# Two k steps of the modulation matmuls between hand-overs, where one was made

## The chip, the cores and the metric

One core of a Trainium2 chip runs the whole program. The metric is the device time of one execution in microseconds (us). The kernel before took 1104.37 us, the median of three runs (1100.53 to 1105.21).

## The reference, cut to what matters

Two layers of a diffusion backbone over 256 latent and 256 context tokens of width 1024. Each layer computes

- a modulation: `mod = silu(c) @ w_mod[l] + b_mod[l]`, the same for `c_ctx`; `w_mod[l]` is 1024 x 6144, and the result is cut into six vectors `sh1, sc1, g1, sh2, sc2, g2`;
- `h = rmsnorm(x) * (1 + sc1) + sh1`, one combined input projection, then attention (8 heads) and a chunked SSD scan side by side, an output projection, and `x + g1 * o`;
- `h2 = rmsnorm(x) * (1 + sc2) + sh2`, a router, 32 experts of which two are used per token, and `x + g2 * y`.

In the second layer only the latent tokens go on. A final norm closes it. All data are float32.

## The kernel before, in words

**Modulation.** The vectors `sh1` and `sc1` of a layer are made by `mod_norm1`. The other four are made by `mod_group`, two groups per layer (`i` = 1 gives `g1, sh2`; `i` = 2 gives `sc2, g2`). A group contracts over 1024 in eight k steps. A k step is one 1 MB chunk of `w_mod` (128 x 2048) and four matmuls (line 303), one for each 512 columns, into four strips of 32 partitions of one PSUM bank (`md`, one buffer). A float32 matmul leaves two records in the trace, so a step is eight records, and the 32 steps of the kernel are 256. After the eighth step the bias is added (line 307), the result goes to DRAM, and four transposes (line 316) bring it into columns.

**Generators.** `mod_group` is a generator: after each k step it yields, with its estimated cost 0.94, and the caller decides what is emitted next. There are three callers' ways.

- `weave` (line 335) runs several generators together and always advances the one whose summed cost over its weight is least. In both layers the attention (`g_att`), the SSD (`g_ssd`) and the modulation (`mods`) are woven so (line 991), with weights 70, 28, 28 in layer 0 and 45, 15, 18 in layer 1. In layer 0 all its modulation groups are in this weave: two of `mod_group` and then `mod_norm1` of layer 1.
- `take(mods, n)` (line 348) advances it n yields. Layer 1 uses it: one, one and three yields (`EARLY - 2`) while its first norm waits for the last sums of the layer before (lines 521, 528, 546), and then `MBULK[n]` yields after each yield of the `bulk` generator (line 984), which makes the projections: `MBULK` is 1 at n = 0, 2, 4, 6 and 8, and 0 elsewhere.
- what is left in layer 1 goes into its weave.

So in layer 1 the five `take` yields are the steps k = 0 to 4 of its first group, the five of `MBULK` are k = 5, 6, 7, the bias and the transposes, and the eight steps of its second group are in the weave.

**Where the chunks lie.** Chunks k = 0 to 4 of layer 1's first group (`EARLY = 5`) are loaded early into large buffers (`wm`). The next five chunks of layer 1 (`MSMALL = 5`) are loaded by `qload` as four 256 KB quarters into small buffers whose tags are given by `MTAGS` ("pppt" and "tyyx"); these are tags that attention and SSD use as well. `chunk(k + 1, True)` asks for such a chunk one step ahead. All other chunks are loaded by `rload` into the tag `wh`, which has four buffers of 1 MB (`WHB = 4`).

**The four `wh` buffers.** The projections' weights are split into a high and a low part (`split_next`, lines 381 and 382: ScalarE makes the high part, VectorE the low one), and each such pair takes two of the four `wh` buffers. `weights(i)` at the head of each pair of blocks asks for the pair after the next. `bulk` goes through six blocks of `xbc` (three pairs) and then two passes of `z` (a pair each). After it, `wkv` and `wq` (lines 986, 987) take `wh` buffers, and hold them to the end of the attention.

**What sets the order.** The framework orders each engine's instructions when the program is built: it goes by program order, takes what its own time estimate says is ready, and gives a freed buffer to the one that asked first. `pin(...)` keeps some instructions in program order; inside `manual_schedule` the listed engines keep the order written. DMAs are issued on SyncE's queue (SP), in order; one that waits for a buffer holds up those behind it.

Of the kernel before, what the change touches and what calls it, by code (L numbers as in the profile page):

```python
# [82 lines left out]
def _tile_kernel(tc, A, out, dbg=None):  # L83
    nc = tc.nc
    pin = tc.keep_in_program_order
    V, S, G, T = nc.vector, nc.scalar, nc.gpsimd, nc.tensor
# [21 lines left out]
    def tp():  # L108
        return psT.tile([128, 512], F32, tag="tp", name="tp")

    def md_():
        return psM.tile([128, 512], F32, tag="md", name="md")
# [10 lines left out]
    def tw(tag, bufs, name, dt=F32):  # L123
        return P.tile([128, 512], dt, tag=tag, name=name, bufs=bufs)
# [9 lines left out]
    def rload(src, shape, t=None, after=None):  # L134
        n = 1
        for s in shape[1:]:
            n *= s
        v = (wh("wl") if t is None else t)[:, :n]
        if after is not None:
            V.tensor_copy(v[:, 0:1], after)  # L140
        d = nc.sync.dma_start(v, src)
        if pinned[0]:
            pin(d)
        if len(shape) == 3:
            v = v.rearrange("p (a b) -> p a b", a=shape[1])
        return v
# [15 lines left out]
    csT = kc[:, KC_A:KC_A + 256].rearrange("p (k m) -> p k m", k=8)  # L162
# [51 lines left out]
    def mod_norm1(l, pre=()):  # L214
        a1 = cp.tile([128, 2, 8], F32, tag="a1", name="a1", bufs=2)
        b1 = cp.tile([128, 2, 8], F32, tag="b1", name="b1", bufs=2)
        modT[l, "a1"], modT[l, "b1"] = a1, b1
        for b in range(8):
            w = pre[b] if b < len(pre) else rload(A["wm0"][l, b], [128, 8, 256], big("wm") if pre else None)
            pm = md_()  # L220
            for k in range(8):
                g = k % 4
                T.matmul(pm[32 * g:32 * g + 32, 0:256], csT[:, k, :], w[:, k], start=(k < 4), stop=(k >= 4))
            mr = tw("bm", 2, "mr")[:, 0:256]
            V.tensor_copy(mr, pm[:, 0:256])
            yield 0.9
            pt = tp()
            for s in range(2):
                T.matmul(pt[:, 2 * s:2 * s + 2], mr[:, s * 128:(s + 1) * 128], kcs("sel"), start=True, stop=True)
            V.tensor_scalar(b1[:, :, b], pt[:, 0:2], cps("bsh", l)[:, b:b + 1], None, op0=ALU.add)  # L230
            V.tensor_scalar(a1[:, :, b], pt[:, 2:4], cps("bsc", l)[:, b:b + 1], 1.0, op0=ALU.add, op1=ALU.add)
            V.tensor_scalar(a1[:, :, b], a1[:, :, b], cps("n1g", l)[:, b:b + 1], None, op0=ALU.mult)
            yield 0.1

    def qload(src, tags, after=None):
        q = []
        for n, a in enumerate(tags):
            if a == "o":
                t = kcs("rope")
            elif a == "k":  # L240
                t = kd[:, 0:512]
            elif a == "w":
                t = ke[:, 0:512]
            elif a == "l":
                t = kc[:, KC["le"][0]:KC["le"][0] + 512]
            elif a == "s":
                t2 = sm([128, D], "sact")
                t = t2[:, 0:512]
            elif a == "a":
                t = t2[:, 512:1024]  # L250
            else:
                tag, bufs = QUARTER[a]
                t = P.tile([128, 520], F32, tag=tag, name="we", bufs=bufs)[:, 0:512] if a == "q" else tw(tag, bufs, "we")
            if after is not None:
                G.tensor_copy(t[:, 0:1], after)
            nc.sync.dma_start(t, src[:, n * 512:(n + 1) * 512])
            q.append(t)
        return q
# [10 lines left out]
    def mod_group(l, i, pre=()):  # L269
        if i == 0:  # L270
            yield from mod_norm1(l)
            return
        pm = md_()
        q = {}

        def chunk(k, ahead=False):
            if k not in q and k < 8:
                src = A["wmod"][l, i - 1, k]
                if k < len(pre):
                    q[k] = [pre[k][:, g * 512:(g + 1) * 512] for g in range(4)]  # L280
                elif l and nmod[0] < MSMALL:
                    q[k] = qload(src, MTAGS[k % 2])
                    nmod[0] += 1
                elif not ahead:
                    w = rload(src, [128, 2048])
                    q[k] = [w[:, g * 512:(g + 1) * 512] for g in range(4)]
            return q.get(k)

        for k in range(8):
            if k == BMK:  # L290
                bm = tw("bm", 2, "bm")
                pin(G.memset(bm, 0.0))
                for who in range(2):
                    pin(nc.scalar.dma_start(bm[who:who + 97:32, :], A["bmod"][l, i]))
                if i == 2:
                    n2 = tw("bm", 2, "n2")
                    pin(G.memset(n2, 0.0))
                    for who in range(2):
                        pin(nc.scalar.dma_start(n2[who:who + 33:32, :], A["n2r"][l]))
            w = chunk(k)  # L300
            chunk(k + 1, True)
            for g in range(4):
                T.matmul(pm[32 * g:32 * g + 32, :], csT[:, k, :], w[g],
                         start=(k == 0), stop=(k == 7))
            yield 0.94
        mr = bm
        V.tensor_tensor(mr, pm, bm, op=ALU.add)
        if i == 2:
            V.scalar_tensor_tensor(mr[0:64], mr[0:64], 1.0, n2[0:64], op0=ALU.add, op1=ALU.mult)
        dt_ = dp.tile([128, 512], F32, tag=f"modd{l}{i}", name=f"modd{l}{i}")  # L310
        nc.gpsimd.dma_start(dt_[:], mr)
        modd[l, i] = dt_
        yield 0.01
        pt = tp()
        for b in range(4):
            T.transpose(pt[:, b * 128:(b + 1) * 128], mr[:, b * 128:(b + 1) * 128], ident)
        pv = pt.rearrange("p (b s h r) -> p r s h b", b=4, s=2, h=2)
        sec, nm = ((1, "sh2"), (0, "a2"))[i - 1]
        d = cp.tile([128, 2, 8], F32, tag=nm, name=nm)
        modT[l, nm] = d  # L320
        for who in range(2):
            V.tensor_copy(d[:, who].rearrange("p (h b) -> p h b", h=2), pv[:, who, sec])
        yield 0.5
# [38 lines left out]
    def mixer(l):  # L362
# [4 lines left out]
        pinned[0] = PINM[l]  # L367
        early = [rload(A["wmod"][l, MODS[l][0][1] - 1, k], [128, 2048], big("wm")) for k in range(EARLY * l)]
        mods = chain(*[mod_group(*m, early if i == 0 else ()) for i, m in enumerate(MODS[l])])
        hT, hH, hL, xn = [], [], [], []  # L370
        wsrc = [A["wt"][l, 0], A["wt"][l, 1], A["wxbc"][l, 2], A["wxbc"][l, 0], A["wxbc"][l, 1], A["wz"][l, 0], A["wz"][l, 1]]
# [1606 lines left out]
```

## Time and profile before

| | |
|---|---|
| median of three runs | 1104.37 us |
| the profiled execution's own time | 1102.8 us |
| its span | 1101.0 us |
| TensorE (PE) busy | 1009.9 us, 92% |
| VectorE (DVE) busy | 608.9 us, 55% |
| ScalarE (ACT), GpSimd (POOL) busy | 334.8 us, 355.0 us |
| mean granted TensorE clock | 0.968 |
| DMA moved | 306.21 MB, 278 GB/s mean |

The stages in the trace: projections of layer 0 up to about 118 us; its weave to about 256; its output projection, router and experts to about 634; layer 1's norm and projections to 718; its weave to about 800; then its output projection, router and experts to the end. In a timeline row the columns are start, duration, engine, line, operation, tile written <- tiles read, shapes, and the number of instructions merged; a bracket gives idle time of the engine ahead of it and what ended it.

### The profile page before, as it was taken

The numbers are of one execution on the slowest core, as the hardware profiler recorded it, in microseconds if no ns is written. First come the engines' busy times: TensorE is split into PE (matmuls) and PEld (weight loads), VectorE is DVE, ScalarE is ACT, GpSimd is POOL, SyncE is SP. The second block draws the span as 40 slices with busy tenths as digits, with TensorE's granted clock in tenths as the row PEclk, the third lists the DMA queues.
The fourth block names the chain that finished last, engine by engine and source line by source line (L and its number), as shares of the span: only waits on it lengthen the run. The fifth ranks groups of instructions, "written<-read, shape, count | busy, mean of one in ns | idle before, by whom it ended". The sixth has DMA issues, their size and how long they took to land. (4 is left out here: it accounts for less than half of the span.)

```text
span 1101.0 us, 14498 instructions
## 1 busy us (share of the span) xinstructions
PE 1009.9 (92%) x5244; PEld 558.0 (51%) x5244; DVE 608.9 (55%) x1351; ACT 334.8 (30%) x688; POOL 355.0 (32%) x366
## 2 busy tenths in 40 slices
PE   5999999999996999999699889999997999899986
PEld 3778554667674344344244357845775344323321
DVE  4596288875785356556445677749864153222222
ACT  4464344544630111111012075434642111101101
POOL 2130134420562467667636431023311011111121
PEclk9999999999986999999899899999997999999998
DMA  9521577787287997999979164475679699898971
GB/s 375 180 77 52 206 261 257 248 335 311 97 295 293 368 367 318 415 418 404 382 283 418 43 235 155 151 288 212 244 269 329 238 388 420 337 372 356 420 265 39
DMA packets 54675, 306.21 MB, mean 278 GB/s; under 512 B 6168, under 2 KB 7064, under 8 KB 22976
## 3 DMA queue, kind: packets, MB, share of 16 engines
q1 hardware_dynamic: 49120, 288.10, 67.0%
q0 software_dynamic: 4224, 15.21, 4.5%
q10 hardware_dynamic: 1248, 1.86, 0.5%
q8 instruction: 44, 0.72, 0.3%
q14 instruction: 39, 0.32, 0.1%
HBM read 300.89 MB, written 4.26 MB: 277 GB/s over the span
## 5 line engine op out<-in xcount | busy, mean ns | idle before, releaser
L1678 POOL TENSOR_TENSOR xs<-xs,tmp 128x512 f32<-128x512 f32 x144 | 180.2, 1281 | 276.4 <-DVE tmp L1677 276.3
L1610 PE MATMUL bk<-we,xgT 128*64 128x512 f32 (+1 forms) x950 | 242.1, 602 | 0.0
L1610 PEld LDWEIGHTS bk<-we,xgT 128*64 128x64 f32 (+1 forms) x950 | 62.7, 125 | 130.4 <-issue 127.9
L1647 PE MATMUL sc<-we,sa 128*64 128x512 f32 (+1 forms) x430 | 106.2, 600 | 0.1
L1663 DVE SCALAR_TENSOR_TENSOR yl<-sc,gs,yh 128x512 fp32r<-128x512 f32 x46 | 34.3, 748 | 113.2 <-ACT yh L1662 112.6
L1662 ACT ACTIVATE yh<-sc,gs 128x512 fp32r<-128x512 f32 x46 | 31.5, 687 | 210.9 <-PE sc L1647 167.7
L1647 PEld LDWEIGHTS sc<-we,sa 128*64 128x64 f32 (+1 forms) x430 | 31.1, 125 | 58.0 <-issue 56.7
L1677 DVE TENSOR_TENSOR tmp<-md,g 128x512 f32<-128x512 f32 x60 | 41.3, 688 | 29.7 <-POOL xs L1678 18.7
L1677 DVE TENSOR_TENSOR tmp<-py,g 128x512 f32<-128x512 f32 x60 | 41.2, 687 | 24.0 <-PE py L1674 13.2
L1616 ACT ACTIVATE sa<-bk 128x256 f32<-128x256 f32 x24 | 9.2, 383 | 136.1 <-PE bk L1610 126.8
L1578 PEld LDWEIGHTS tp<-PT,h 128*128 128x128 f32 x256 | 33.9, 199 | 28.4 <-issue 12.7
L1578 PE MATMUL tp<-PT,h 128*128 128x128 f32 x256 | 41.5, 300 | 5.0 <-DVE PT L1500 1.7
L770 PE MATMUL sc<-kT,qT 128*128 128x512 f32 (+1 forms) x96 | 45.7, 559 | 0.0
L792 PE MATMUL py<-pT,vt 128*64 128x128 f32 x320 | 43.6, 280 | 1.2 <-DVE oT L821 1.2
L1072 DVE TENSOR_TENSOR lo<-wo,hi 128x512 fp32r<-128x512 f32 x44 | 34.4, 785 | 16.2 <-PE sc L1255 8.6
L1584 DVE TENSOR_SCALAR xgT<-tp,a,sh 128x128 f32<-128x128 f32 x32 | 13.0, 409 | 54.1 <-PE tp L1578 47.5
L1582 ACT ACTIVATE xgT<-tp,sh,a 128x128 f32<-128x128 f32 x32 | 14.6, 457 | 91.0 <-PE tp L1578 85.2
L792 PEld LDWEIGHTS py<-pT,vt 128*64 128x64 f32 x320 | 32.5, 136 | 15.4 <-issue 8.2
L401 PE MATMUL bk<-wh,hH 128*128 128x256 f32 (+1 forms) x128 | 39.8, 311 | 0.2
L403 PE MATMUL bk<-wh,hL 128*128 128x256 f32 (+1 forms) x128 | 38.2, 298 | 1.8 <-DVE hL L382 1.7
L774 ACT ACTIVATE p<-sc,mx 128x512 f32<-128x512 f32 (+1 forms) x48 | 29.4, 612 | 33.2 <-DVE mx L772 23.2
L402 PE MATMUL bk<-wl,hH 128*128 128x256 f32 (+1 forms) x128 | 37.8, 295 | 0.0
(421 smaller groups left out, 2146.5 us busy)
## 6 DMA issues: line engine op xcount, KB each, us to landing
we<-wgu SPq DMA_DIRECT2D x111, 1024.0 KB, 11.1
we<-wdn SPq DMA_DIRECT2D x53, 1024.0 KB, 9.8
wl<-wmod SPq DMA_DIRECT2D x22, 1024.0 KB, 4.9
wl<-wm SPq DMA_DIRECT2D x10, 1024.0 KB, 8.2
wo<-wout SPq DMA_DIRECT2D x8, 1024.0 KB, 5.8
we<-wgu SPq DMA_DIRECT2D x31, 256.0 KB, 5.3
ring<-wgu SPq DMA_DIRECT2D x7, 1024.0 KB, 5.8
wm<-wm SPq DMA_DIRECT2D x6, 1024.0 KB, 12.2
```

The source lines that it names most:

```text
L401: T.matmul(o, a[0], b[0], start=start, stop=False)
L402: T.matmul(o, a[0], b[1], start=False, stop=False)
L403: T.matmul(o, a[1], b[0], start=False, stop=stop)
L770: T.matmul(pm[:, 0:nk], qT[:, e, t * 128:(t + 1) * 128], kT[:, e, 0:nk], start=True, stop=True)
L792: T.matmul(py[e * 64:(e + 1) * 64, 0:128], vts[0][:, k, h * 64:(h + 1) * 64], pT[:, k * 128:(k + 1) * 128], start=(k == 0), stop=(k == nk ...
L1072: eng.tensor_tensor(lo, src, hi.bitcast(F32), op=ALU.subtract)
L1578: T.matmul(p_, R["hres"][t][:, c], xg[j], start=(j == 0), stop=(j == nT - 1))
L1610: T.matmul(pg[c], xgT[b][half][:, k, c], w[i][k], start=(half == 0 and k == 0), stop=(half == 1 and k == 3))
L1647: T.matmul(pd[h][c], aT[:, k, c], w[i][2 * k + h], start=(k == 0), stop=(k == 1))
L1663: V.scalar_tensor_tensor(yl, pd[h], gs[:, b:b + 1], yh.bitcast(F32), op0=ALU.mult, op1=ALU.subtract)
L1677: V.tensor_tensor(tmp, pc, g2[1 if t < 2 else 0][h], op=ALU.mult)
L1678: (eng or (V if EADD[l][n] == "V" or alt and n % 2 else G)).tensor_tensor(xs[:, t, hs_], xs[:, t, hs_], tmp, op=ALU.add)
```

## The change

The loop over k goes in steps of two. Both chunks are asked for first, then the chunk after them (which only `qload` chunks follow), then all eight matmuls are emitted, and the generator yields once, with cost 1.88. `take` and `MBULK` count yields and keep their numbers.

```diff
-        for k in range(8):
+        for k in range(0, 8, 2):
             if k == BMK:
                 bm = tw("bm", 2, "bm")
...
-            w = chunk(k)
-            chunk(k + 1, True)
-            for g in range(4):
-                T.matmul(pm[32 * g:32 * g + 32, :], csT[:, k, :], w[g],
-                         start=(k == 0), stop=(k == 7))
-            yield 0.94
+            ws = [chunk(k), chunk(k + 1)]
+            chunk(k + 2, True)
+            for n, w in enumerate(ws):
+                for g in range(4):
+                    T.matmul(pm[32 * g:32 * g + 32, :], csT[:, k + n, :], w[g],
+                             start=(k + n == 0), stop=(k + n == 7))
+            yield 1.88
```

## Rows read from the trace of the kernel before

**Rows 1.** The page's busy time of each engine (share of the span).

```profile
PE 1009.9 (92%) x5244; PEld 558.0 (51%) x5244; DVE 608.9 (55%) x1351; ACT 334.8 (30%) x688; POOL 355.0 (32%) x366
```

**Rows 2.** Instructions of line 303: durations min/median/max in ns, first and last start.

```profile
L303 PE MATMUL md<-wl,kc x176: 592/593/618, 127.8 to 757.0; 128*32 128x512 f32 x176
L303 PE MATMUL md<-wm,kc x40: 592/593/1062, 635.5 to 646.3; 128*32 128x512 f32 x40
L303 PE MATMUL md<-we,kc x40: 592/605/617, 676.6 to 728.2; 128*32 128x512 f32 x40
```

**Rows 3.** Busy time of each engine in two stretches of layer 1's weave.

```profile
718.00:757.00 39.00, 37.84 (x186) 16.03 (x188) 24.27 (x58) 16.22 (x38) 12.07 (x13) 1.00 0.71 269
757.00:800.00 43.00, 40.68 (x252) 30.14 (x245) 38.31 (x86) 23.31 (x56) 15.02 (x16) 1.00 0.65 236
```

**Rows 4.** The same for layer 0's weave, without `mod_norm1`'s part.

```profile
118.00:208.00 90.00, 87.84 (x473) 44.98 (x472) 67.61 (x165) 43.75 (x114) 32.95 (x34) 1.00 0.71 258
```

**Rows 5.** Timeline of PE at the head of layer 1.

```profile
635.47 1.07 PE L303 MATMUL md<-wm,kc 128*32 128x512 f32 x8
638.56 0.69 PE L490 MATMUL tp<-kc,xn 128*128 128x128 f32 x2 [2.03 <-DVE xn L495]
...
642.22 0.44 PE L490 MATMUL tp<-kc,xn 128*128 128x128 f32 x2 [0.49 <-DVE xn L495]
...
644.15 2.78 PE L303 MATMUL md<-wm,kc 128*32 128x512 f32 x24
647.34 1.11 PE L435 MATMUL tp<-kc,xn 128*128 128x128 f32 x8 [0.41 <-DVE hf L447]
```

**Rows 6.** Timeline of PE around one modulation step in layer 1's projections.

```profile
682.06 0.39 PE L403 MATMUL bk<-hH,wl 128*128 128x512 f32 x1
682.38 1.07 PE L303 MATMUL md<-we,kc 128*32 128x512 f32 x8
683.37 0.50 PE L401 MATMUL bk<-hH,wh 128*128 128x512 f32 x1
683.71 0.39 PE L402 MATMUL bk<-hL,wh 128*128 128x512 f32 x1
683.94 0.39 PE L403 MATMUL bk<-hH,wl 128*128 128x512 f32 x1
```

**Rows 7.** Timeline: who takes the wh buffers at the end of the projections.

```profile
692.87 1.06 ACT L381 ACTIVATE wh<-ring 128x1024 fp32r<-128x1024 f32 x1
...
705.16 1.06 ACT L381 ACTIVATE wh<-ring 128x1024 fp32r<-128x1024 f32 x1 [0.19 <-PE bk L402]
...
705.98 0.37 PE L401 MATMUL bk<-wh,hH 128*128 128x256 f32 x1
...
706.58 2.35 DVE L382 TENSOR_TENSOR wl<-ring,wh 128x1024 fp32r<-128x1024 f32 x2
...
711.88 0.33 SPq L141 DMA_DIRECT2D wl<-wkvb  x1
...
718.14 1.02 PE L737 MATMUL bk<-wl,kvqa 128*128 128x512 f32 x2
718.21 0.33 SPq L141 DMA_DIRECT2D wl<-wmod  x1
```

**Rows 8.** DMA issues of 640 to 760 us (count, size, median us to landing).

```profile
wl<-wmod SPq DMA_DIRECT2D x6, 1024.0 KB, 4.8
```

**Rows 9.** Timeline of PE in layer 0: a step, and the one two steps later.

```profile
147.82 1.07 PE L303 MATMUL md<-wl,kc 128*32 128x512 f32 x8
...
155.04 1.07 PE L303 MATMUL md<-wl,kc 128*32 128x512 f32 x8
```

**Rows 10.** PE idle before layer 1, and the clock of the stretch around it.

```profile
623.52 1.11 PE L1647 MATMUL sc<-ring,sa 128*64 128x512 f32 x1 [2.54 <-DVE sa L1625]
```

**Rows 11.** Busy time of that stretch; the last three columns are clock, DMA share, GB/s.

```profile
621.00:628.00 7.00, 4.48 (x12) 1.40 (x14) 3.64 (x7) 0.69 (x1) 1.79 (x2) 0.54 0.01 2
```

**Rows 12.** Who waited for whom from 672 to 800 us, the longest.

```profile
POOL yt L921 <- PE md L303: 28.5, 1, 28.5
```

## The prediction

> **What bounds the kernel now.** I read the page's busy shares first: PE is busy 92% of the span [rows 1], so the kernel is bound by PE's work, and an edit that adds and removes no matmul can move the time only by what PE idles, by what a change of stream costs it, and by its clock. Next I read where the changed line runs [rows 2]. Its 256 records are 32 steps: 16 in layer 0's weave, and in layer 1 the five `wm` steps at the head, and then up to 757 us. Then I read the busy time of the stages that hold them. Layer 0's weave has PE busy 87.84 of 90 us [rows 4], layer 1's 37.84 of 39 us while modulation steps are left and 40.68 of 43 us when there are none [rows 3]. So little idle can be won: 2.16 us in layer 0 and 3.48 us in layer 1. The timelines last, for the head of layer 1 and for the four `wh` buffers.
>
> **What the change does.** Matmuls, bytes and the work of the other engines stay. Three things change.
>
> *Fewer hand-overs.* In the three-step run at 644.15 a step takes 2.78 / 3 = 0.93 us [rows 5]. A step by itself takes 683.37 - 682.38 = 0.99 us, and its neighbours lose a little: from the matmul before to the step 0.32 us, from the one behind to the next 0.34 us, where matmuls of that stream follow each other in 0.23 us [rows 6]. A hand-over saved is thus worth 0.06 + 0.09 + 0.11 = 0.26 us at most; in a weave, where the streams change anyway, perhaps nothing. Layer 0 can lose 8 of its 16 visits. Layer 1 goes from 14 (k0, k1, the run of three, k5 to k7 and eight) to about eight. That bounds the gain by 14 x 0.26 = 3.6 us. In layer 0 a chunk's buffer comes free only with the step two before it (`wkv` and `wq` hold the other two), and from the end of one step to the start of the one two later I read 155.04 - (147.82 + 1.07) = 6.1 us at the least [rows 9], of which the load is most. Chunks therefore arrive one at a time, and many pairs will still run as two visits. I take half: 7 x 0.23 = 1.6 us gained (0 to 3.6).
>
> *The takes count double.* This I hold for the larger part. `take` and `MBULK` count yields, and a yield is now two steps. At the head of layer 1 the first yield makes k0 and k1, the second k2 and k3, the third k4 and k5, and the two after it k6, k7 and the bias. The extra k1 (0.93 us) lies in the 2.03 us of idle up to 638.56, the extra k3 in the time up to 642.22, when the next transposes wait for VectorE [rows 5]. In exchange only k4 is left for the run at 644.15, and its place is open until 647.34 unless k5's chunk has landed: five steps are hidden by these waits before and five or six after. I take nothing (a gain of 0.9 us if k5 fits; a loss of 1.5 us if the emptier stretch lets the clock fall). Then `MBULK`'s five yields are the transposes of the first group and all eight steps of the second, which were in the weave. So 8 x 0.93 = 7.4 us of PE work leaves layer 1's weave and enters its projections. The two cancel, but for the waits on either side.
>
> *The wait that this adds.* Of the second group's chunks only k0 and k1 are quarter loads; k2 to k7 go to `wh`, and now they ask for it in the middle of the projections, where the four buffers are passed from one split pair to the next with no slack. I read this in [rows 7]: the split for the last pass (705.16) waits for the last matmul of the pair before it, `wkv` is issued at 711.88 when the first z pass releases its pair, and the old k2 load at 718.21, when the second does. The chain with the change, counted from the end of the second `xbc` pair (T, about 692.9 before, where the next split starts [rows 7]), with 6.1 us from a free buffer to its step [rows 9]:
>
> - T: the freed pair goes to chunks k2 and k3. They run at about T + 6.5 and T + 8, and the pair goes to the split for z's first pass. From the start of a split to the end of the low part is 706.58 + 2.35 - 705.16 = 3.8 us [rows 7], so it is ready at T + 11.8. PE has the third pair for 705.16 - 692.87 = 12.3 us and the two steps, 1.9 us: no stall.
> - T + 13.7 or so: the third pair's buffers go to k4 and k5 (steps at T + 20 and T + 21.5). The first z pass takes 711.88 - 705.98 = 5.9 us, to T + 19.6; its buffers go to k6 and k7, which asked ahead of the last split. That split gets k4's and k5's buffers at T + 22.5 and gives z's second pass its first half some 1.3 us later. PE does two steps in these 4.2 us: 2.3 us open.
> - z's second pass and k6, k7 end at about T + 31.6; `wkv` gets k6's buffer at about T + 27, lands 4.8 us later by the loads of that stretch [rows 8], and with the same 6.1 us is used at T + 33: 1.4 us open.
>
> That is 3.7 us. What can stand in: SSD's first matmuls need no `wh` buffer, and the order is by readiness. They are few at that point, so I take 2.0 us lost (0 if all is filled; 9 us if each of the three loads comes 2 us later than I count and the clock falls once).
>
> *What the weave loses.* Without the filler its idle share is that of the second stretch, 2.32 of 43 us (5.4%), not 1.16 of 39 (3.0%) [rows 3]. The 37.84 - 7.4 = 30.4 us that stay take 32.2 us instead of 31.3: 0.8 us lost (0 to 3). For layer 0's order, which the planner makes anew, I take nothing (2 us either way, the idle it has [rows 4]).
>
> **Sum.** -1.6 + 0 + 2.0 + 0.8 + 0 = +1.2 us on the profiled execution's 1102.8 us, thus 1104.0. That execution lies 1.6 us under the median of the runs, 1104.4, so for a median I predict 1105.6 us.
>
> One rule of the Trainium skill speaks against the change. The trace first: after 2.54 us of idle at 623.5 [rows 10] the clock of 621 to 628 us was 0.54 in the mean, near the lower level of 1.2 GHz, with 4.48 us of PE work in it [rows 11], so that one such idle cost about 2 us beyond itself. The page "TensorE: Matmul & The Clock Gate", section "HAM oscillation", says that waits for loads between short bursts of matmuls make the gate halve the clock each time, so that the next burst starts slow. By it the two openings that I count before and behind z's second pass would each bring about 2 us more, and the sum would be +5.2; by the row alone, openings of 2.3 and 1.4 us are shorter than the one that did it.
>
> **Rivals.**
>
> *Slower: the buffer chain starves z.* The same chain, unfilled, 3.7 us; 1 us more for each of three loads, since the projections' own loads share the queues, 3 us; half clock after the two openings at the price of [rows 10, 11], 2 x 2 us; less the 1 us of hand-overs that remain: about +9.5 us, 1114. It decides from the point where k5's load lands after the end of z's first pass. For it: the four buffers have no slack [rows 7]. Against: SSD work can fill in, and layer 0 runs on two buffers with PE 98% busy [rows 4].
>
> *Faster: SSD starts earlier.* The second group's k0 and k1 now run before the weave and give back their small buffers; before, GpSimd's first `yt` waited 28.5 us for line 303 [rows 12]. If SSD's VectorE and GpSimd work then moves under the projections, nothing is open in the chain, the 3.48 us of idle in the weave go, and all 3.6 us of hand-overs are won: -7 us, 1097. Against: SSD reads the blocks that the projections have only just made, and VectorE is busy 38.31 of 43 us in the weave's second part [rows 3], which a filler never caused.
>
> *It does not do what it says.* Loads, not yields, set where the steps run; pairs run apart, and the takes' shift is hidden: 1104.4.
>
> **How the numbers follow.** About 0.5% (5.5 us) is what a measurement of this kernel can tell from no change. My forecast gets 0.40, the pairs that run apart 0.13, both within that; the starved chain 0.31, faster 0.16. The chance of same is 0.40 + 0.13, less 0.04 that the forecast's own spread (1099 to 1112) puts beyond the bound: 0.49. Slower: 0.31 + 0.04 = 0.35. Faster 0.16. The range reaches to the rivals' prices and a little beyond the slower one, whose bounds are wider: 1097 to 1117.
>
> **What would show it.** Right: line 303 ends near 726 us, not 757; loads of `wmod` into `wl` in layer 1 at about 695, 708 and 715 us, not from 718; the first L737 some 8 us later than 718.1; the weave from there to 800 shorter by about 6.5 us. The starved chain: PE idle of over 3 us ahead of z's second pass or L737, and a clock under 1.00 between 710 and 735. Faster: no idle there, and the weave shorter by over 9 us. Wrong altogether: line 303 still running beyond 750 us, or a difference that comes up in layer 0's weave or in the experts, which I count at nothing.

## The result, and the profile after

The changed kernel takes 1117.67 us (median of 7 runs, 1114.5 to 1122.43) where the kernel before took 1101.81 us beside it (7 runs, 1098.13 to 1110.32): a ratio of 1.0126, interval 1.0096 to 1.0156, so some 14 us slower (10.6 to 17.2). This ratio, like those in the table below, is the one on record for the two sets of runs; the quotient of the two medians would be 1.0144. The profiled execution took 1122.43 us, the slowest of the seven, so its own difference (19.7 us of span) is larger than that of the medians. Every line below the loop has moved down by one: line 303 is 304 after, 737 is 738.

The page's busy shares after, which answer to [rows 1]:

```profile
PE 1019.1 (91%) x5244; PEld 560.4 (50%) x5244; DVE 609.7 (54%) x1351; ACT 336.3 (30%) x688; POOL 357.3 (32%) x366
```

The instructions are the same in number, yet PE is busy 9.2 us more: part of the loss is matmuls that take longer, not idle time. The changed line after, against [rows 2]:

```profile
L304 PE MATMUL md<-wl,kc x176: 592/592/617, 130.5 to 742.0; 128*32 128x512 f32 x176
L304 PE MATMUL md<-wm,kc x40: 592/592/617, 641.5 to 650.5; 128*32 128x512 f32 x40
L304 PE MATMUL md<-we,kc x40: 592/593/1063, 655.9 to 701.8; 128*32 128x512 f32 x40
```

All of it has started by 742.0, before the weave; the quarter chunks (`we`) now run from 655.9, at the head, where before they began at 676.6. To see what each stage pays, I cut both traces at the same instructions. **Head** is from the first line 1749 (1750 after), layer 0's last sums, to the last transpose of line 712 (713); **projections** from there to the last line 737 (738); **weave** from there to the last line 960 (961). Busy times of the three, before:

```profile
629.50:672.30 42.80, 37.74 (x214) 26.70 (x212) 30.48 (x52) 26.14 (x57) 13.52 (x20) 0.96 0.51 177
672.30:721.20 48.90, 47.41 (x282) 37.22 (x281) 33.79 (x69) 23.12 (x37) 2.37 (x11) 1.00 0.52 190
721.20:789.90 68.70, 65.22 (x356) 37.05 (x354) 54.66 (x121) 31.75 (x76) 26.11 (x26) 1.00 0.65 243
```

and after (PE is the first engine column; the last three are clock, DMA share, GB/s; the fourth row is a piece of the head):

```profile
635.50:690.40 54.90, 47.72 (x238) 28.33 (x236) 31.92 (x53) 26.71 (x57) 14.22 (x22) 0.94 0.56 197
690.40:748.90 58.50, 54.09 (x322) 38.37 (x321) 35.66 (x70) 23.50 (x37) 6.96 (x14) 1.00 0.57 215
748.90:812.90 64.00, 58.23 (x303) 37.52 (x302) 51.52 (x119) 31.20 (x74) 21.93 (x21) 0.97 0.37 142
651.50:657.50 6.00, 2.61 (x8) 0.91 (x8) 5.08 (x7) 3.86 (x7) 0.00 (x0) 0.50 0.83 293
```

Head +12.1, projections +9.6, weave -4.7: +17.0 us. The rest is +2.7 up to layer 0's weave, +3.3 in layer 0 and -3.3 behind layer 1's weave; these three vary as much between kernels that do not differ there (below).

**The head.** PE's timeline after, against [rows 5]:

```profile
641.49 1.92 PE L304 MATMUL md<-wm,kc 128*32 128x512 f32 x16
...
644.52 1.92 PE L304 MATMUL md<-wm,kc 128*32 128x512 f32 x16
...
649.99 1.06 PE L304 MATMUL md<-wm,kc 128*32 128x512 f32 x8
654.89 1.12 PE L436 MATMUL tp<-kc,xn 128*128 128x128 f32 x4 [3.84 <-DVE hf L448]
655.94 1.92 PE L304 MATMUL md<-we,kc 128*32 128x512 f32 x4
...
658.83 1.05 PE L304 MATMUL md<-we,kc 128*32 128x512 f32 x2
...
662.81 1.05 PE L304 MATMUL md<-we,kc 128*32 128x512 f32 x4
...
672.19 1.04 PE L304 MATMUL md<-we,kc 128*32 128x512 f32 x2
```

Two things are to be seen. Only k4 is left at 649.99, where three steps stood in a row before, and 3.84 us of idle follow (0.41 before); the clock of 651.5 to 657.5 is 0.50, the lower level of 1.2 GHz. Then k5, k6 and k7 come, which the prediction's sums had left in the projections, and they come in pieces of two or four records: nine pieces up to 672.19 that take some 9.7 us (each from its start to the next matmul's), where three whole steps take 2.78 us [rows 5]. A piece of two records (one matmul of 512 columns into one strip) takes 1.05 us, as long as the eight records of a whole step (1.06 us at 649.99): the four strips of a step run beside each other, and a strip alone pays the whole. The Trainium skill, page "TensorEngine Tiling (Array Packing)", section "Key Properties", says that tiles operate independently and can execute in parallel; these rows agree, and add what is lost when a quarter of a step runs by itself.

The fall of the clock is not new at the head. Before, it came at k1, after the 2.03 us of idle at 636.5 [rows 5], and k1 took 1.94 us. Its row in PE's timeline, and the busy times of that stretch with the clock:

```profile
639.18 1.94 PE L303 MATMUL md<-wm,kc 128*32 128x512 f32 x8
638.50:642.00 3.50, 3.17 (x12) 0.78 (x12) 1.35 (x3) 0.87 (x4) 2.96 (x7) 0.51 0.17 42
```

Why the opening lasts longer can be read on VectorE, before

```profile
644.80 2.03 DVE L382 TENSOR_TENSOR wl<-ring,wh 128x864 fp32r<-128x864 f32 x2 [1.08 <-ACT wh L381]
646.75 0.99 DVE L447 TENSOR_SCALAR hf<-tp,a,b 128x256 f32<-128x256 f32 x2
```

and after:

```profile
650.41 2.03 DVE L383 TENSOR_TENSOR wl<-ring,wh 128x864 fp32r<-128x864 f32 x2 [0.85 <-ACT wh L382]
652.36 2.02 DVE L383 TENSOR_TENSOR wl<-wr,wh 128x864 fp32r<-128x864 f32 x2
654.30 0.99 DVE L448 TENSOR_SCALAR hf<-tp,a,b 128x256 f32<-128x256 f32 x2
```

The two splits of the second weights (`wr`) stand ahead of the `hf` for which the transposes of line 436 wait. Of the 3.43 us by which the opening grows (3.84 - 0.41), about half is this: from k4's start to line 436 it is 4.90 us (649.99 to 654.89), where from the start of the three steps it was 3.19 (644.15 to 647.34), 1.71 us more. The other 1.72 us is that one step stands in the opening and not three; that half is idle, but it does not move the time at which the wait ends.

**The projections.** Against [rows 7], the second group's chunks from `wh`, PE after:

```profile
716.69 1.06 PE L304 MATMUL md<-wl,kc 128*32 128x512 f32 x8 [1.05 <-DMA wl<-wmod]
...
734.74 0.44 PE L617 MATMUL tp<-kc,acc 128*128 128x128 f32 x2 [0.99 <-ACT acc L613]
...
738.06 1.06 PE L304 MATMUL md<-wl,kc 128*32 128x512 f32 x8 [1.28 <-DMA wl<-wmod]
...
741.51 1.06 PE L304 MATMUL md<-wl,kc 128*32 128x512 f32 x8
...
745.84 1.45 PE L738 MATMUL bk<-wl,kvqa 128*128 128x512 f32 x3
```

and SP's queue there:

```profile
710.63 0.80 SPq L141 DMA_DIRECT2D wl<-wmod  x2
...
725.99 0.80 SPq L141 DMA_DIRECT2D wl<-wmod  x2
733.26 0.80 SPq L141 DMA_DIRECT2D wl<-wmod  x2
739.18 0.33 SPq L141 DMA_DIRECT2D wl<-wkvb  x1
```

The chain is there: chunks are asked for in three lots of two as buffers come free, `wkv` behind them, and PE waits up to 1.28 us for a chunk. The first chunk of a lot ends PE's wait 6.1 us after its issue (k2, 716.69 - 710.63) and 4.8 us (k6, 738.06 - 733.26); the trace has the landing of one of the six alone, the second of the last lot, after 6.8 us, where [rows 8] has 4.8 for loads issued one at a time.

### The profile page after: what moved, and what is told of

It is laid out like the page before. It is cut to its first block, busy times and chain, and to the rows that moved or that the text cites. A ratio compares the mean times of both kernels' runs of the same rounds, so it can differ in the third digit from the quotient of the medians.

```text
span 1120.7 us, 14485 instructions
## 1 busy us (share of the span) xinstructions
PE 1019.1 (91%) x5244; PEld 560.4 (50%) x5244; DVE 609.7 (54%) x1351; ACT 336.3 (30%) x688; POOL 357.3 (32%) x366
## 5 line engine op out<-in xcount | busy, mean ns | idle before, releaser
L1648 PE MATMUL sc<-we,sa 128*64 128x512 f32 (+1 forms) x430 | 102.5, 600 | 0.1
## 6 DMA issues: line engine op xcount, KB each, us to landing
we<-wdn SPq DMA_DIRECT2D x53, 1024.0 KB, 10.6
```

Source lines behind the costliest of these rows:

```text
L1648: T.matmul(pd[h][c], aT[:, k, c], w[i][2 * k + h], start=(k == 0), stop=(k == 1))
```

## The experiments

Each was timed beside the kernel before (5 to 12 runs each), and one execution of each was profiled. All but the two with whole chunks and the one with six early chunks share one form of the loop, which hands over the tuples that `parts_` gives:

```diff
+    one = [(j,) for j in range(8)]
+    two = [(0, 1), (2, 3), (4, 5), (6, 7)]
-        for k in range(8):
+        for ks in parts_(l, i):
...
+            ws = [chunk(j) for j in ks]
+            chunk(ks[-1] + 1, True)
...
+            yield 0.94 * len(ks)
```

Below, each edit is against the kernel before unless it says otherwise. Stage lengths (us) are of that one execution, cut in every trace at the same instructions; "layer 0" is from its first value projection (line 737) to the head, "experts" layer 1's last stage, from the last line 1110 to the start of PE's last matmul.

| kernel | ratio (interval) | layer 0 | head | proj. | weave | experts |
|---|---|---|---|---|---|---|
| before | | 510.3 | 42.8 | 48.9 | 68.7 | 262.9 |
| changed | 1.0126 (1.0096-1.0156) | 513.6 | 54.9 | 58.5 | 64.0 | 260.3 |
| pairs in layer 0 | 1.0035 (1.0016-1.0053) | 515.7 | 43.6 | 49.0 | 68.6 | 262.6 |
| pairs in layer 1 | 1.0121 (1.0094-1.0147) | 510.4 | 54.9 | 58.0 | 63.8 | 257.3 |
| pairs, same reach | 1.0003 (0.9984-1.0021) | 516.0 | 46.2 | 48.5 | 67.4 | 258.4 |
| singles, far reach | 1.0120 (1.0095-1.0146) | 513.4 | 54.9 | 58.1 | 63.8 | 257.3 |
| far at the head only | 1.0065 (1.0038-1.0092) | 510.4 | 54.9 | 45.7 | 68.0 | 260.7 |
| far in the bulk only | 1.0102 (1.0072-1.0133) | 512.0 | 42.8 | 66.2 | 63.7 | 257.5 |
| whole chunks, group 1 | 1.0078 (1.0048-1.0107) | 513.6 | 47.9 | 59.5 | 65.0 | 257.7 |
| six early chunks | 1.0044 (1.0022-1.0066) | 513.8 | 46.1 | 47.6 | 69.3 | 260.4 |
| all chunks whole | 1.0027 (1.0002-1.0051) | 516.9 | 48.1 | 55.0 | 63.7 | 257.4 |
| layer 0, shifted pairs | 1.0008 (0.9983-1.0033) | 513.0 | 42.8 | 48.9 | 68.7 | 263.0 |
| group 2 pairs | 0.9954 (0.9926-0.9981) | 510.3 | 42.9 | 48.6 | 68.1 | 257.9 |
| group 2 shifted pairs | 0.9938 (0.9915-0.9962) | 511.9 | 42.8 | 48.7 | 65.3 | 260.2 |

**Which layer: pairs in layer 0 alone, pairs in layer 1 alone.**

```diff
+        return two if l == 0 else one      # layer 0 alone
+        return two if l else one           # layer 1 alone
```

> Pairs in layer 0 only, layer 1 as before. Theory A (the wh buffer chain in layer 1's projections costs the time, as the prediction had it) and theory B (the head of layer 1 costs it: k5 to k7 are now taken there, from quarter loads, and their matmuls are split up): both 0, within 0.3%. Theory C (layer 0's weave, whose stage was about 3 us longer in the changed trace, carries a part): +3 us, 0.3%.

> Pairs in layer 1 only, layer 0 as before. A and B: all of the loss, +14 us (1.2 to 1.3%). C: +10 to +11 us.

Measured 1.0035 and 1.0121. Layer 1 alone brings the whole loss, as A and B had it; layer 0 alone takes a third of a per cent, as only C had it, and together they took no more than layer 1 alone.

**The reach or the pairing.** One kernel makes pairs but sets the takes back so that each reaches as few steps as before; the other makes single steps and lets the takes reach as far as the change does.

```diff
+        return [(0, 1), (2, 3), (4,), (5, 6), (7,)] if (l, i) == (1, 1) else two
-            take(mods, EARLY - 2)
+            take(mods, 1)
+MBULK = (1, 0, 0, 0, 1, 0, 1, 0, 1, 0, 0, 0, 0, 0)
```

```diff
+        return one
-                take(mods, 1)
+                take(mods, 2)      # both; the third: take(mods, 5)
+MBULK = (1, 0, 2, 0, 2, 0, 2, 0, 2, 0, 0, 0, 0, 0)
```

> Pairs in both layers, but every take of layer 1 reaches the step that it reached before: the head ends with k4, the projections hold k5 to k7 and the bias of the first group, the second group is in the weave, as pairs. A and B: the loss is gone, 0 within 0.4%; saved hand-overs could give up to -2 us. If pairing itself costs (two loads must be there, the weave is coarser): +5 us or more.

> Single steps everywhere, but the takes of layer 1 reach as far as they do with the change: k0 to k7 and the bias at the head, the whole second group in the projections. A and B: the loss is there without any pair, +10 to +14 us. If pairing itself costs: 0 to +4 us.

Measured 1.0003 and 1.0120, against 1.0121 for pairs in layer 1. These two settle that the reach alone brings the whole loss, and that pairs without it cost nothing on balance. The balance has parts of both signs in the profile: layer 0 +5.7 us and the head +3.4, the weave -1.3 and the experts -4.5.

**Where the reach costs: the head or the bulk.** Single steps, the far reach in one place at a time.

```diff
+MBULK = (1, 0, 0, 0, 0, 0, 0, 0, 0, 0, 0, 0, 0, 0)   # head only; takes 2, 2, 5
+MBULK = (2, 2, 3, 0, 2, 0, 2, 0, 2, 0, 0, 0, 0, 0)   # bulk only; takes as before
```

> Single steps; only the takes at the head of layer 1 reach farther (k0 to k7 and the bias there), the projections take the transposes alone, and the second group is in the weave as before. A (buffer chain in the projections): 0 to +2 us. B (split matmuls of k5 to k7 and a slow clock at the head): +6 to +10 us, with line 303 or its like taking about 1 us of PE for one matmul, where four together take 0.93.

> Single steps; the head ends with k4 as before, and only the takes in the projections reach farther (k5 to k7 early in them, then the whole second group, k2 to k7 of it in wh buffers). A: +4 us or more, with PE idle ahead of z's second pass and of the value projection. B: at most +2 us.

Measured 1.0065 and 1.0102. Both cost. That the bulk alone would cost 2 us at most was a miss: with eleven steps in it the projections are 20.5 us longer than with none (45.7), and eleven steps are 10.9 us of work. Of the rest, 2.8 us are idle (66.20 - 61.68, less 1.69), and two of the eleven steps, whose chunks are quarters, ran in three pieces each:

```profile
675.40:741.60 66.20, 61.68 (x346) 39.04 (x345) 36.91 (x71) 23.59 (x37) 7.56 (x15) 1.00 0.64 238
```

The head alone is 12.1 us longer, of which 2.8 us are the three steps that it takes over. The projections without any step:

```profile
682.70:728.40 45.70, 44.01 (x258) 36.81 (x257) 32.96 (x68) 23.27 (x37) 1.65 (x10) 1.00 0.36 134
```

This is the measure for the stage: 1.69 us idle, 45.7 us.

**What the head pays for: quarters or the opening.** The changed kernel, with the first group's k5 to k7 loaded whole into large buffers; and the changed kernel with a sixth early chunk and takes that go no further.

```diff
+                elif (l, i) == (1, 1):
+                    w = rload(src, [128, 2048], big("wm"))
+                    q[k] = [w[:, g * 512:(g + 1) * 512] for g in range(4)]
+                    nmod[0] += 1
```

```diff
+EARLY = 6
+MBULK = (1, 0, 1, 0, 1, 0, 0, 0, 0, 0, 0, 0, 0, 0)
-            take(mods, EARLY - 2)
+            take(mods, 1)
```

> The changed kernel, but chunks 5 to 7 of layer 1's first group are loaded whole, 1 MB each, into large buffers (those that k0 to k4 give back), so that the four matmuls of a step become ready together. B: about 6 us faster than the changed kernel, that is +7 to +9 us on the kernel before. A: no different from the changed kernel, +14 us.

> Pairs, with six chunks loaded early instead of five, so that the head holds three whole pairs (k0 to k5), the projections hold k6, k7 and the bias, and the second group is in the weave. A and B: no loss, -3 to +3 us on the kernel before. If the sixth early chunk delays the head's weight loads: +3 us or more.

Measured 1.0078 and 1.0044. With whole chunks the head falls by 7.0 us, to 47.9, and its three last steps stand whole in PE's timeline, of which the first and the last are shown (line 304 is 308 there):

```profile
652.97 1.97 PE L440 MATMUL tp<-kc,xn 128*128 128x128 f32 x8 [3.84 <-DVE hf L452]
660.64 1.06 PE L308 MATMUL md<-wm,kc 128*32 128x512 f32 x8
...
667.38 1.06 PE L308 MATMUL md<-wm,kc 128*32 128x512 f32 x8
```

So the quarters' pieces cost 7.0 us, as read (9.7 - 2.8 = 6.9). The opening of 3.84 us stays; it is the 2.3 us that remain of 47.9 - 42.8 - 2.8. Six early chunks were expected to lose nothing, or 3 us and more if the sixth load delays the head's own, and lost 0.44%: the head is 3.3 us longer for one more step and one quarter of k6, and PE's wait of 3.21 us there is again for `hf`. The head is not all of that loss: this kernel has pairs in layer 0 too, which is 3.5 us longer. The opening is in every head that takes k2 and k3 ahead: pairs with the same reach, whose head makes the same five steps as before and one quarter of k5 at the lower clock, take 3.4 us more (the stage, and that quarter in PE's timeline),

```profile
634.50:680.70 46.20, 38.58 (x215) 27.13 (x214) 30.49 (x52) 26.29 (x57) 13.49 (x20) 0.93 0.49 170
655.37 1.92 PE L311 MATMUL md<-we,kc 128*32 128x512 f32 x2
```

with 7.62 us of idle in the stage where before had 5.06 and a clock of 0.93 for 0.96. Heads with single takes (far in the bulk only, layer 0 shifted, both kernels with pairs in group 2) stay at 42.8 or 42.9. With pairs in layer 0 alone the head is as before but for the clock: the three steps k2 to k4 take 5.14 us at the lower one,

```profile
649.41 5.14 PE L311 MATMUL md<-wm,kc 128*32 128x512 f32 x24
```

VectorE keeps the order of before there, and the head is 43.6 us, 0.8 more. So a slow clock at this place costs about 0.8 us where `hf` is not late. That VectorE's order of splits makes up most of the rest was read, not tried.

**What the projections pay for.** As whole chunks for group 1, but for all of layer 1 (the condition is `elif l:`), so that no chunk goes through `wh` or in quarters.

> The changed kernel, with every chunk of layer 1 from the head's k5 on loaded whole into the large buffers that hold the early chunks, none in quarters and none in the four wh buffers. Theory A (the projections lose 4.9 us to the wh chain and to quarters run singly): head near 48 us as with whole chunks for the first group alone, projections near 45.7 + 8 x 0.99 = 53.6 us (58.5 with the change), median 5 us under that of whole chunks for the first group alone, ratio 1.003. Theory B (the projections lose because eight steps there displace the stage's own loads and order, wherever the chunks land): projections stay at 57 us or more, ratio 1.007 or above.

Measured 1.0027, against 1.0078 for group 1 alone (1107.13 and 1111.36 us). The projections go from 59.5 to 55.0 with all eight steps in them, each a run of eight records, and no idle of PE for one of them:

```profile
684.00:739.00 55.00, 53.50 (x323) 37.80 (x321) 34.94 (x71) 23.58 (x37) 5.32 (x15) 1.00 0.70 269
```

The idle of the stage is 1.50 us where the change has 4.41. Against the changed kernel that is 2.9 of the 3.5 us by which the stage is shorter; the chain of `wh` buffers was most of its loss, and eight steps there cost little else (55.0 - 45.7 - 7.9 = 1.4 us, about the 8 x 0.20 us that neighbours lose to a step by [rows 6]).

**Layer 0.** Another grouping of its steps: k0, k1+k2, k3+k4, k5+k6, k7.

```diff
+    two = [(0,), (1, 2), (3, 4), (5, 6), (7,)]
```

> The kernel before, with layer 0's steps handed over as k0, k1+k2, k3+k4, k5+k6, k7 and layer 1's one at a time. Theory A (giving two steps at once in layer 0 costs time by itself, since steps run one by one as their loads land): slower by about 0.35%, 4 us, as the pairs k0+k1, k2+k3, ... in layer 0 alone, with layer 0's weave 2 us longer or more. Theory B (what layer 0 loses is the chance of one order that the planner made): another order, anywhere within 0.3% of before on either side, and the weave of layer 0 as long as before.

Measured 1.0008, with layer 0 2.7 us longer than before in the profile, not 5.4. The trace of the changed kernel shows what pairs do here: the steps still run one by one, as their chunks land,

```profile
139.34 1.06 PE L304 MATMUL md<-wl,kc 128*32 128x512 f32 x8
...
142.19 1.06 PE L304 MATMUL md<-wl,kc 128*32 128x512 f32 x8
...
150.47 1.06 PE L304 MATMUL md<-wl,kc 128*32 128x512 f32 x8
...
157.70 1.06 PE L304 MATMUL md<-wl,kc 128*32 128x512 f32 x8
```

at the same distances as before (136.7, 139.5, 147.8 and 155.0), so that no hand-over is saved: line 303 has 17 visits (unbroken runs on PE) in layer 0 before and 18 after. What pairs change is the order of everything else. A price of giving two steps at once in layer 0 is not shown, then; that the 0.35% go with one order is likely, but the two intervals overlap. Layer 0 also came out at 512 to 513 us in kernels that changed nothing in it, so I explain none of its differences.

**Pairs where no take reaches further.** Only the second group of layer 1, which is all in the weave. A second kernel has the same line, with `two` as in the last edit for layer 0.

```diff
+        return two if (l, i) == (1, 2) else one
```

> The kernel before, with pairs in layer 1's second group alone, whose steps are all taken in layer 1's weave; no take reaches further than before. Theory A (the reach of the takes is what costs, and a pair by itself saves at most its hand-overs): within 0.2% of before, at best 4 x 0.26 = 1.0 us faster; the head stays at 42.8, the projections at 48.9, the weave at 68.7 us or up to 1 us less. Theory B (pairs by themselves cost something in a weave, as layer 0's alone did with 0.35%): 2 to 4 us slower, all of it in the weave.

> The kernel before, with layer 1's second group handed over as k0, k1+k2, k3+k4, k5+k6, k7 (pairs k0+k1, k2+k3, ... in that group alone measured 0.9954, of whose 8 us in the profile 5.0 lay in layer 1's expert stage, which holds no modulation step). Theory A (pairs themselves save time in the weave): the weave 0.5 us shorter than before or more, and by the same route the median again 4 to 5 us below before, ratio near 0.995. Theory B (the gain is that of another order which the planner made downstream): the weave and the projections within 0.5 us of before, and the expert stage at one of the lengths seen so far (257 to 263 us); the ratio follows that stage alone, 1.000 at 263 and 0.995 at 257.

Measured 0.9954 with k0+k1, k2+k3, ... and 0.9938 with k0, k1+k2, ..., k7: both faster than before, about 5 and 7 us, and both beyond what I had allowed for hand-overs (1.0 us). In the first, 5.0 of the 8.0 us of span lie in the expert stage. The second was made to tell the pairs from a chance of order there: its weave is 3.4 us shorter, with 0.81 us of idle where before has 3.48, so part of its gain lies in the weave. The first's weave is 0.6 us shorter, with 1.89 us of idle. Whether the pairs do this, or the order that the planner makes with them, the two kernels do not tell; saved hand-overs are not it, for line 303 has 16 visits in layer 1 before, 16 in the first kernel and 14 in the second. The weave of the first, then of the second:

```profile
719.40:787.50 68.10, 66.21 (x360) 37.51 (x358) 50.67 (x120) 32.10 (x76) 26.73 (x26) 1.00 0.61 232
```

```profile
721.90:787.20 65.30, 64.49 (x356) 37.37 (x354) 51.45 (x119) 31.48 (x74) 25.45 (x26) 1.00 0.61 236
```

Of the waits of before that are gone in both, the three longest are:

```profile
762.54 1.13 PE L760 MATMUL bk<-kvqa,wl 128*128 128x256 f32 x4 [0.70 <-DVE yi L955]
764.60 0.66 PE L316 MATMUL tp<-kc,bm 128*128 128x128 f32 x4 [0.56 <-DVE bm L309]
785.01 1.13 PE L953 MATMUL bk<-hs,bcb 128*128 128x256 f32 x4 [1.06 <-DVE qT L763]
```

By the rule that only the expert stage counts, its 260.2 us would have given about 0.9975 to the second; 0.9938 is below that. Which of the weave's new positions removes the waits stays open, and so does how much of the expert stage's 2.7 and 5.0 us is order and how much clock.

## Why the prediction was wrong in its likeliest case, by its steps

The forecast was 1105.6 us, no change; measured against the 1104.4 us of the runs shown the ratio gives 1118.3 us, slower by more than the bound, 1.3 us above the range's upper end (1117), and near the price of the first rival (1114). Its terms, layer 1's from the stages:

| term | forecast | measured |
|---|---|---|
| hand-overs saved | -1.6 | none: 33 visits of line 303 before, 38 after |
| head | 0 | +9.3 (12.1 less 2.8 of moved work) |
| chain in the projections | +2.0 | +4.9 (58.5 - 45.7 - 8 x 0.99) |
| weave | +0.8 | +3.2 (7.9 - 4.7) |
| layer 0's order | 0 | +3.3 in the profile; 0 to 4 us timed |

- **The takes count double** was right, as was its place as the larger part: single steps with that reach cost 1.0120, pairs without it 1.0003. `wmod` was asked for at 710.6, 726.0 and 733.3, line 303's last record at 742.0 and the first line 738 at 745.8. Less the 18.1 us by which the projections begin later (690.4 against 672.3) these are 692.5, 707.9, 715.2, 723.9 and 727.7, where the prediction had 695, 708, 715, 726 and some 726: it saw the course of the projections to within 2.5 us.
- **The head, "I take nothing", is the step that failed.** The prediction counted "five steps are hidden by these waits before and five or six after" and set its loss at 1.5 us at most. It had read itself that the third take reaches k6, k7 and the bias, so that eight steps come there, but not that k5 to k7 are quarter loads whose matmuls can be run one at a time. Measured, 7.0 us of pieces and 2.3 us of opening. The opening at 644.15 was looked at rightly: "a loss of 1.5 us if the emptier stretch lets the clock fall" is the case that came, with 3.84 us of idle and a clock of 0.50. But the clock had fallen at the head before, too (0.51 at 638.5), and most of the 2.3 us is that `hf` comes 1.71 us later. The extra k1 and k3 were hidden, as it said: from the first step to k4 the head takes 8.50 us with four steps, where it took 8.68 with two.
- **"So 8 x 0.93 = 7.4 us of PE work leaves layer 1's weave and enters its projections. The two cancel"** overlooked that k5 to k7 leave the projections for the head. The projections gain five steps, not eight.
- **The buffer chain** was the right mechanism and undersized. Unfilled I had 3.7 us and took 2.0; measured were 2.7 us of idle (4.41 against 1.69) and 2.2 us more of busy PE than the 7.9 of the steps (54.09 - 44.01 - 7.9), of which whole chunks took back 0.6 (53.50); the other 1.6 us are the 8 x 0.20 us that neighbours lose to a step by [rows 6], which the term left out. The openings came elsewhere than forecast: 1.05 us at k2, in the third `xbc` pair, where the chain had no stall, 0.99 us for a transpose that waited for ScalarE, 1.28 us at k6, and none ahead of the value projection. SSD's early matmuls did not fill them.
- **The weave** lost 3.2 us against 0.8 (the bound was 3): with no filler the idle is 5.77 of 64.0 us. The first SSD matmuls wait 2.16 us for GpSimd, and the second group of them runs slower (1.10 us, where the first takes 0.65); the clock of 759 to 763 us was 0.71:

```profile
759.43 0.65 PE L895 MATMUL bk<-xw,bcb 128*64 128x256 f32 x4 [2.16 <-POOL xw L892]
760.62 1.10 PE L895 MATMUL bk<-xw,bcb 128*64 128x256 f32 x4 [0.53 <-POOL xw L892]
```

- **The clock rule** did not decide where it was weighed: the openings in the projections, 1.05, 0.99 and 1.28 us, left the clock at 1.00. The clock fell at the head, where the prediction had allowed 1.5 us for it but put nothing into its sum, and it fell there before the change, too: the 2.03 us of [rows 5], shorter than the opening of 2.3 us that the prediction called "shorter than the one that did it", had done it as well. At the head the trace agrees with what the prediction takes from the Trainium skill, page "TensorE: Matmul & The Clock Gate", section "HAM oscillation", though PE waited there for VectorE and not for a load.
- **Two slips of the sum**, which change nothing: 7 x 0.26 is 1.8, where 7 x 0.23 was taken, and 30.4 us at the second stretch's idle share take 32.1 us, not 32.2.
- **The rivals.** That the range nearly held the result is luck: its upper end was set by a rival whose mechanism was not the main one. The starved chain came out in size (1114) but mostly by another cause; of its parts the openings and the later loads did occur in the projections, the clock's fall after them did not, and the head was not in it. Of "It does not do what it says" the first half came true, pairs ran apart, and the second did not: the takes' shift was not hidden. The faster one fell: `yt` no longer waits 28.5 us for line 303 [rows 12] but 21.2 us for VectorE:

```profile
POOL yt L922 <- DVE xt L618: 21.2, 1, 21.2
```

## What to carry to other kernels

When a generator's grain changes, recount everything that counts its yields: here the numbers in `take` and `MBULK` were the whole loss, and pairs with the takes left where they were came out between 0.6% faster and 0.35% slower. Before moving a step earlier, look at how its data come: a step whose operands land in quarters, and whose matmuls share the array only when they run together, can cost three times its price when it is run as the quarters land. A filler has its place by the wait that it covers; spent earlier, it leaves that wait bare. Then ask what ends the wait: here it was VectorE, whose order had changed too.

## What the runs showed of the hardware that I had not expected

One matmul into a strip of 32 columns keeps PE as long (1.05 us for its two records) as four of them into four strips (1.06 us for eight).

The clock does not follow from the rows just ahead of it alone. Ahead of line 1720 in the expert stage, before and the kernel with pairs in group 2 have the same waits (0.83 us, then 1.73 us) and the same matmuls; in the first the clock falls to 0.57 in the next 4 us, in the second it stays at 1.00. Before, the matmuls behind the second wait, and the stretch from 0.5 us after its end:

```profile
1071.52 1.57 PE L1720 MATMUL bk<-xs,kc 128*128 128x512 f32 x2 [1.73 <-POOL xs L1678]
1072.00:1076.00 4.00, 4.00 (x12) 0.70 (x12) 0.00 (x0) 0.00 (x0) 0.69 (x1) 0.57 0.00 0
```

and pairs in group 2, the same two:

```profile
1065.13 1.12 PE L1728 MATMUL bk<-xs,kc 128*128 128x512 f32 x2 [1.73 <-POOL xs L1686]
1065.60:1069.60 4.00, 4.00 (x18) 0.96 (x18) 0.00 (x0) 0.00 (x0) 0.69 (x1) 1.00 0.00 0
```

That is one way in which stages with the same instructions come to differ between kernels, and why I put no single stage's difference of that size down to an edit without a second kernel that shows it.
